# Moved operands and weights at fixed distances modulo 256 bytes: two kinds of slots in a one-core decoder step

## The chip, the cores and the metric

The kernel runs on one core of a Trainium2 chip. The metric is the device time of one execution in microseconds (us); lower is better. Times come from the runs and from one execution that the hardware profiler took.

## What is computed

One inference step of a one-layer decoder over 288 tokens: a prompt of 256 and 8 samples of 4 tokens. All is fp32. The reference, cut to the parts that matter here:

```python
mod = (silu(c) @ w_ada + b_ada)            # 6 vectors of 2048 for each of 9 groups
h = _rms(x, g_mix) * (1 + sc_m) + sh_m
proj = h @ w_in                            # 2048 -> 9216, split in seven
...                                        # short gated convolution; chunked spatial gating
merged = sigmoid(ga) * (ya @ w_pa) + sigmoid(gb) * (yb @ w_pb)
x = x + gt_m * (merged @ w_out)
h2 = _rms(x, g_ffn) * (1 + sc_f) + sh_f
gate, up = split(h2 @ w_ffn_in)            # 2048 -> 2 x 5632
x = x + gt_f * ((silu(gate) * up) @ w_ffn_out)
```

## The kernel before

Activations lie transposed: 128 features on the partitions, 288 tokens along the free axis. A matmul keeps a 128x128 piece of weights in the array and moves 128x288 of activations through it into one PSUM buffer (L229 to L234, in `triple`). For accuracy every fp32 operand is split in a high part (rounded to the format fp32r) and a low part (the rest), and a product is three matmuls: high weights with the high operand (L229), high weights with the low operand (L232), low weights with the high operand (L234). Each loads its weights anew.

The weights stream from HBM as blocks of up to 1 MB into seven `raw` buffers, on SP's queue in program order. For every four pieces, ScalarE (ACT) casts the high part into a `hi` tile (L453) and VectorE (DVE) subtracts for a `lo` tile (L459); there are four tiles of 2,048 bytes a partition of each (`SPB`). The moved operands are split likewise by `split` (L301, L303) and by `modulate` and `make_h1`, into tiles of the pool `slots`, named `s` in the profile.

The pool has 92 slots, all alike: they hold moved operands, but also evicted results, the partial sums of w_in (`part`) and small constants. A slot has room for `TU` = 298 columns, because the first stages move ten columns beside the tokens. The allocator rounds 1,192 bytes up to 1,216, so that slots begin at 32, 96, 160 or 224 modulo 256; the `hi` and `lo` tiles all begin at 224.

The order: conditioning vectors (`ada`, L393: fp32 matmuls spread over the stages), w_in in passes over parts of the depth (`wA`, `wB`, `wX`, `wS`, `wC`, `wE`, `wF`, `wD`), mixers, `pa`, `pb`, `wo`, then the FFN (`fk`, `fi`, and `f0` to `f3`). TensorE's order is written out by hand in the whole kernel. ACT, DVE and SP are recorded by hand in the first stages and are otherwise placed by the scheduling layer, which makes an instruction that writes a reused slot wait until its last reader is done.

In the first pass `sinkA` evicts each output tile from PSUM, for the first 48 (`ROOTLESS`) with the ten extra columns; `sinkC` and `rescale` read these columns later, once the root of the norm is known.

## Time and profile before

| | |
|---|---|
| median of 3 runs | 1624.26 us (1624.0 to 1624.49) |
| profiled execution | 1624.22 us, its span 1622.4 us |
| mean granted TensorE clock | 0.998 |
| TensorE busy | 1611.5 us, 12641 matmuls |
| DVE busy, ACT busy | 1017.0 us, 737.3 us |
| DMA | 357.88 MB, mean 221 GB/s |

The span runs from the first instruction to the last. A row of a group names source line, engine, operation and tiles (written <- read), then the shape and the count, busy time and the mean duration of one in ns. In a row of a window the columns are PE, PEld (weight loads), DVE, ACT and POOL busy in us with instruction counts, then the granted clock, the DMA share and GB/s; asked for one engine, it has that engine's column alone. Matmuls overlap: the next starts before the one ahead has drained, so the distance between starts (the pitch) is less than the duration of one.

### The profile page before, as it was taken

The numbers are of one execution on the slowest core, as the hardware profiler recorded it, in microseconds if no ns is written. First come the engines' busy times: TensorE is split into PE (matmuls) and PEld (weight loads), VectorE is DVE, ScalarE is ACT, GpSimd is POOL, SyncE is SP. The second block draws the span as 40 slices with busy tenths as digits, with TensorE's granted clock in tenths as the row PEclk, the third lists the DMA queues.
The fourth block names the chain that finished last, engine by engine and source line by source line (L and its number), as shares of the span: only waits on it lengthen the run. The fifth ranks groups of instructions, "written<-read, shape, count | busy, mean of one in ns | idle before, by whom it ended". The sixth has DMA issues, their size and how long they took to land.

```text
span 1622.4 us, 31579 instructions
## 1 busy us (share of the span) xinstructions
PE 1611.5 (99%) x12641; PEld 1547.6 (95%) x12641; DVE 1017.0 (63%) x2194; ACT 737.3 (45%) x1360; POOL 21.2 (1%) x65
## 2 busy tenths in 40 slices
PE   9999999999999999999999999999999999999997
PEld 8998999899999999999999999999999999999997
DVE  6676788877755667667744555555555555555565
ACT  5533344643444434456643444444444444444454
POOL 0000000000000000011000000000000000000000
PEclk9999999999999999999999999999999999999999
DMA  9887866777778676654576556443564534645341
GB/s 376 324 319 287 312 237 212 273 279 295 288 281 337 260 271 227 236 176 157 193 304 251 217 177 208 159 172 110 169 224 156 173 117 161 226 157 172 109 162 59
DMA packets 59476, 357.88 MB, mean 221 GB/s; under 512 B 6720, under 2 KB 10176, under 8 KB 28608
## 3 DMA queue, kind: packets, MB, share of 16 engines
q1 hardware_dynamic: 59040, 355.73, 59.8%
q8 instruction: 99, 1.62, 0.4%
q14 instruction: 49, 0.40, 0.1%
q10 hardware_dynamic: 288, 0.13, 0.0%
HBM read 352.74 MB, written 3.09 MB: 219 GB/s over the span
## 4 chain that ended last, share of the span: by engine, by line
PE 98%; DMA 1%; DVE 0%; ACT 0%; DVEq 0%; issue 0%; ACTq 0%
PE pm L229 31%; PE pm L234 30%; PE pm L232 30%; PE ada L393 5%; DMA raw<-in_wK 1%; DMA raw<-in_w 0%; DVE st L1048 0%; DMA ct<-in_c 0%; PE px L232 0%; PE px L229 0%; PE px L234 0%; PE px L880 0%; PE px L879 0%; PE px L826 0%; PE px L203 0%; ACT hi L453 0%
## 5 line engine op out<-in xcount | busy, mean ns | idle before, releaser
L229 PE MATMUL pm<-s,hi 128*128 128x288 f32 (+1 forms) x3750 | 1109.1, 296 | 0.0
L232 PE MATMUL pm<-s,hi 128*128 128x288 f32 (+1 forms) x3750 | 1103.8, 294 | 0.0
L234 PE MATMUL pm<-s,lo 128*128 128x288 f32 (+1 forms) x3738 | 1102.2, 295 | 0.0
L453 ACT CAST hi<-raw 128x512 fp32r<-128x512 f32 (+1 forms) x963 | 587.2, 612 | 803.3 <-PE pm L232 762.6
L459 DVE TENSOR_TENSOR lo<-raw,hi 128x512 fp32r<-128x512 f32 (+1 forms) x849 | 578.7, 683 | 437.9 <-ACT hi L453 425.3
L229 PEld LDWEIGHTS pm<-s,hi 128*128 128x128 f32 x3750 | 705.7, 188 | 15.2 <-issue 13.0
L232 PEld LDWEIGHTS pm<-s,hi 128*128 128x128 f32 x3750 | 704.7, 188 | 0.0
L234 PEld LDWEIGHTS pm<-s,lo 128*128 128x128 f32 x3738 | 702.9, 188 | 0.0
L248 DVE TENSOR_TENSOR lo<-raw,hi 128x512 fp32r<-128x512 f32 x111 | 74.6, 675 | 29.6 <-ACT hi L453 28.9
L393 PE MATMUL ada<-raw,cs 128*32 128x512 f32 (+2 forms) x1152 | 88.3, 452 | 0.2 <-DMA raw<-in_a 0.2
L393 PEld LDWEIGHTS ada<-raw,cs 128*32 128x32 f32 x1152 | 30.9, 110 | 45.0 <-issue 41.1
L771 DVE TENSOR_TENSOR s<-pm,s 128x288 f32<-128x288 f32 x72 | 32.8, 456 | 19.9 <-PE pm L234 19.7
L301 ACT CAST s<-t 128x288 fp32r<-128x288 f32 (+1 forms) x76 | 32.9, 433 | 18.8 <-DVE t L803 12.4
L303 DVE TENSOR_TENSOR s<-t,s 128x288 fp32r<-128x288 f32 (+1 forms) x76 | 34.9, 459 | 6.5 <-ACT s L301 6.4
L343 DVE SCALAR_TENSOR_TENSOR x<-pm,mod,x 128x256 f32<-128x256 f32 x79 | 37.6, 475 | 0.0
L969 DVE SCALAR_TENSOR_TENSOR t<-t,pm 128x288 f32<-128x288 f32 x42 | 19.1, 454 | 20.9 <-PE pm L234 20.9
L763 DVE TENSOR_TENSOR s<-pm,s 128x288 f32<-128x288 f32 x48 | 21.8, 454 | 10.4 <-PE pm L234 9.5
L342 DVE TENSOR_TENSOR t<-pm,mod 128x32 f32<-128x32 f32 x79 | 15.2, 192 | 18.3 <-PE pm L234 18.2
L748 DVE SCALAR_TENSOR_TENSOR s<-pm,s 128x256 f32<-128x256 f32 x48 | 23.1, 480 | 4.1 <-PE pm L234 4.1
L754 DVE TENSOR_TENSOR s<-s,rb 128x288 f32<-128x288 f32 x48 | 21.5, 448 | 0.0
L171 ACT ACTIVATE t<-x 128x288 f32<-128x288 f32 x29 | 12.9, 445 | 17.4 <-DVE x L346 17.4
L176 DVE TENSOR_TENSOR acc<-acc,t 128x288 f32<-128x288 f32 x33 | 15.0, 455 | 8.2 <-ACT t L171 8.2
(164 smaller groups left out, 470.9 us busy)
## 6 DMA issues: line engine op xcount, KB each, us to landing
raw<-in_fi SPq DMA_DIRECT2D x84, 1024.0 KB, 4.8
raw<-in_a SPq DMA_DIRECT2D x64, 1024.0 KB, 7.9
raw<-in_f SPq DMA_DIRECT2D x64, 704.0 KB, 4.0
raw<-in_wD SPq DMA_DIRECT2D x34, 1024.0 KB, 5.4
raw<-in_aE SPq DMA_DIRECT2D x16, 1024.0 KB, 9.6
raw<-in_wo SPq DMA_DIRECT2D x16, 1024.0 KB, 6.0
raw<-in_wC SPq DMA_DIRECT2D x19, 768.0 KB, 4.3
raw<-in_pa SPq DMA_DIRECT2D x8, 1024.0 KB, 5.9
```

The lines of the kernel that those rows point to most:

```text
L229: PE.matmul(out, wh, ah, start=first, stop=False)
L232: end_ = PE.matmul(out, wh, al, start=False, stop=turn and last)
L234: end_ = PE.matmul(out, wl, ah, start=False, stop=last)
L248: lows.pop(0)[1]()
L301: A.copy(hi, a)
L303: V.tensor_tensor(lo, a, hi.bitcast(F32), ALU.subtract)
L343: V.scalar_tensor_tensor(x[:, m, :TP], ps[:, :TP], mod[:, gt0 + m, 0:1], x[:, m, :TP], ALU.mult, ALU.add)
L393: PE.matmul(acc[32 * j : 32 * j + 32, :w], cs[:, kt, :], self.raw[:, o : o + w], start=kt == 0, stop=kt == 15, tile_position=(0, 32 * j), ...
L453: A.copy(hi, self.raw[:, s * 128 : e * 128])
L459: sub()
L748: V.scalar_tensor_tensor(t[:, :TP], ps[:, :TP], t[:, T : T + 1], t[:, :TP], ALU.add, ALU.add)
L771: V.tensor_tensor(a, ps[:, :T], a, ALU.add)
```

## The change

The pool of slots becomes two. 56 slots (`MAIN`) of `PITCH` = 320 columns, 1,280 bytes, hold the moved operands and what else is wide; 1,280 is five times 256, so all begin at the same place modulo 256. A moved operand (dtype fp32r) starts 7 columns, 28 bytes, into its slot (`LEADIN`). 36 slots of 288 columns (`KEPT`) hold the partial sums of 36 output tiles of w_in (`LONG`: 24 to 27 and 40 to 71), which live long. The twelve of these that have the ten extra columns put them into small tiles beside: `extra0`, `extra1` and `extra2`, 160 bytes a tile for four of them. `extra0` is allocated between the `hi` and the `lo` tiles and moves the `lo` tiles on by 160 bytes. By the layout of the built program every moved operand then lies 92 bytes from the high weights and 188 from the low ones, modulo 256; before it lay 0, 64, 128 or 192 bytes from both. `ct` and `ctt` move from constants of their own into the ring of temporaries.

```diff
-SLOTS = 92
+MAIN = 56
+KEPT = 36
+LEADIN = 7
+PITCH = 320
...
+LONG = tuple(range(24, 28)) + tuple(range(40, 72))
...
     def slot(dt=F32, shape=(P, T)):
-        return pslot.tile(list(shape), dt, tag="s", name=nm("s"), padded_shape=[P, TU])
+        o = LEADIN if dt == F32R else 0
+        t = pslot.tile([P, o + shape[1]], dt, tag="s", name=nm("s"), padded_shape=[P, PITCH])
+        return t[:, o:] if o else t
+
+    def kept():
+        return pkept.tile([P, T], F32, tag="k", name=nm("s"))
...
-    ct = const("ct", [P, 16, NC])
+    ct = tmp(16 * NC).rearrange("p (k n) -> p k n", n=NC)
...
+    extra, extra2 = [], const("extra2", [P, 4, TU - T])
+
+    def spare():
+        i = len(extra)
+        if i < 2:
+            extra.append(pw.tile([P, 4, TU - T], F32, tag=f"extra{i}", name=f"extra{i}", bufs=1))
...
                 hi = pw.tile([P, w], F32R, tag="hi", name=nm("hi"), bufs=SPB, padded_shape=[P, SEG * 128])
+                spare()
                 A.copy(hi, self.raw[:, s * 128 : e * 128])
                 lo = pw.tile([P, w], F32R, tag="lo", name=nm("lo"), bufs=SPB, padded_shape=[P, SEG * 128])
+                spare()
...
     def sinkA(m, ps):
-        t = slot(shape=(P, TU) if m < ROOTLESS else (P, T))
+        wide = m < ROOTLESS and m not in LONG
+        t = kept() if m in LONG else slot(shape=(P, TU) if wide else (P, T))
         part[m] = t[:, :T]
-        w = T
+        w = TU if wide else T
+        copy = A.copy if (m not in ON_VECTOR if m < ROOTLESS else m % 2 or m % 8 == 4) else V.tensor_copy
+        copy(t[:, :w], ps[:, :w])
         if m < ROOTLESS:
...
+            i = 0 if wide else LONG.index(m)
+            e = t[:, T:] if wide else (extra + [extra2])[i // 4][:, i % 4]
+            raws[m] = t, e
+            if not wide:
+                copy(e, ps[:, T:TU])
...
     def sinkC(m, ps):
...
-        V.scalar_tensor_tensor(t[:, :TP], ps[:, :TP], t[:, T : T + 1], t[:, :TP], ALU.add, ALU.add)
+        V.scalar_tensor_tensor(t[:, :TP], ps[:, :TP], e[:, :1], t[:, :TP], ALU.add, ALU.add)
```

The instructions of TensorE, POOL and SP keep their order and number. ACT and DVE have six more each. On ACT, in the first pass over w_in, this stands before the change; a number in a name counts the allocations of the build.

```order
L453 CAST hi_584<-raw_129 128x512
L740 COPY s_600<-pm_592 128x298
L453 CAST hi_609<-raw_129 128x512
L453 CAST hi_612<-raw_134 128x512
L740 COPY s_615<-pm_602 128x298
L589 ACTIVATE q_123<-x 128x1152
```

And after it:

```order
L471 CAST hi_590<-raw_133 128x512
L758 COPY s_606<-pm_598 128x288
L764 COPY extra_250<-pm_598 128x10
L471 CAST hi_616<-raw_133 128x512
L471 CAST hi_619<-raw_138 128x512
L758 COPY s_622<-pm_609 128x288
L764 COPY extra_250<-pm_609 128x10
L608 ACTIVATE q_127<-x 128x1152
```

Two evictions of output tiles (24 and 25) have become two copies each; all else keeps its place.

The second place is on ACT near the end of the product with w_out (`wo`), where pairs 13 and 14 of the 16 pairs of operands (`xg`) for the first blocks of the FFN are made; here the rows name in brackets what each waits for. Before:

```order
L935 ACTIVATE t_9513<-x,gm_90 128x256
L935 ACTIVATE t_9522<-x,gm_90 128x256 [waits Activation_49]
L301 CAST s_9518<-t_9513 128x298 [waits Activation_49,Pool_49]
L453 CAST hi_9533<-raw_8979 128x512 [waits DMAHW5_49,PE_49]
L301 CAST s_9527<-t_9522 128x298 [waits Activation_49,Pool_49]
L453 CAST hi_9537<-raw_8979 128x512 [waits PE_49]
```

And after:

```order
L957 ACTIVATE t_9531<-x,gm_93 128x256
L957 ACTIVATE t_9540<-x,gm_93 128x256 [waits Activation_49]
L311 CAST s_9536<-t_9531 128x298 [waits PE_49,Activation_49,Pool_49]
L471 CAST hi_9551<-raw_8997 128x512 [waits DMAHW5_49,PE_49]
L311 CAST s_9545<-t_9540 128x298 [waits Activation_49,Pool_49]
L471 CAST hi_9555<-raw_8997 128x512 [waits PE_49]
```

Nothing has moved, but the first cast into a slot now waits for TensorE too.

## The prediction

> **What bounds the kernel now.** I read the page first: its engine table, its slices and the chain that ended last.

> ```profile
> span 1622.4 us, 31579 instructions
> PE 1611.5 (99%) x12641; PEld 1547.6 (95%) x12641; DVE 1017.0 (63%) x2194; ACT 737.3 (45%) x1360; POOL 21.2 (1%) x65
> ...
> PE  9999999999999999999999999999999999999997
> ...
> PEclk9999999999999999999999999999999999999999
> ...
> PE 98%; DMA 1%; DVE 0%; ACT 0%; DVEq 0%; issue 0%; ACTq 0%
> ```

> TensorE is busy in every slice, at the full granted clock, and 98% of the chain lies on it. The waits view asks whether that busy row hides waiting:

> ```profile
> PE pm L576 <- POOL wb L570: 1.1, 1, 1.1
> PE px L203 <- DVE t L185: 0.6, 1, 0.6
> PE px L232 <- DVE s L692: 0.3, 1, 0.3
> ```

> It does not: the three longest waits for another engine come to 2.0 us. So the time is the number of matmuls times the distance from one start to the next. Three groups of the page hold nearly all of them, one for each product of a triple (L229: high weights by high operand, L232: high by low, L234: low by high). Below them is the windows view for a stretch of the FFN that holds only such matmuls.

> ```profile
> L229 PE MATMUL pm<-s,hi 128*128 128x288 f32 (+1 forms) x3750 | 1109.1, 296 | 0.0
> L232 PE MATMUL pm<-s,hi 128*128 128x288 f32 (+1 forms) x3750 | 1103.8, 294 | 0.0
> L234 PE MATMUL pm<-s,lo 128*128 128x288 f32 (+1 forms) x3738 | 1102.2, 295 | 0.0
> ```
> ```profile
> 1160.00:1340.00 180.00, 180.00 (x1363) 1.00 0.48 165
> ```

> 180.00 us over 1363 matmuls is a pitch of 132.1 ns. The groups hold 3750 + 3750 + 3738 = 11,238 matmuls, so 1 ns of pitch is worth 11.2 us. The "mean ns" of a row is longer than the pitch because matmuls are pipelined, but the two move together.

> What would the pitch be if nothing held a matmul up? The kernel contains the answer: the warm-up matmuls of L576 move 288 columns too, in bf16, from one unchanging operand. [...]

> ```profile
> L576 PE MATMUL pm<-wb x10: 286/286/287, 4.4 to 5.5; 128*128 128x288 bf16 x10
> L576 PEld LDWEIGHTS <-wb x8: 97/98/98, 4.6 to 5.4; 128*128 128x128 bf16 x8
> ```
> ```profile
> 4.43 1.14 PE L576 MATMUL pm<-wb 128*128 128x288 bf16 x8
> ```

> Eight matmuls in 1.14 us, the last of them 0.286 long: (1.14 - 0.286) / 7 = 122.0 ns of pitch at a duration of 286. The triples have 132.1 at a mean of (296 + 294 + 295) / 3 = 295. So about 10 ns of each, 113 us in all, is delay that 288 columns do not need by themselves. The line views of 800 to 1600 us show how it varies:

> ```profile
> L229 PE MATMUL pm<-s,hi x1980: 288/294/403, 800.0 to 1599.9; 128*128 128x288 f32 x198
> L232 PE MATMUL pm<-s,hi x1979: 288/295/303, 800.1 to 1599.7; 128*128 128x288 f32 x198
> L234 PE MATMUL pm<-s,lo x1980: 288/295/300, 799.8 to 1599.8; 128*128 128x288 f32 x198
> L229 PEld LDWEIGHTS pm<-s,hi x1980: 186/188/193, 799.8 to 1599.8; 128*128 128x128 f32 x198
> ```

> Each product has cases of 288, nearly free, and cases of 300 and more. Is that chance? A block of the FFN's first half goes through the same 16 pairs of operands in the same order, so I looked at the same two matmuls of a block (the low operand's product of the 14th pair, the first product of the 16th) in blocks 647 us apart, through the groups of a window 1 ns wide: first the one at 874.09 us, then the one at 874.74.

> ```profile
> L232 PE MATMUL pm<-s,hi 128*128 128x288 f32 x1 | 0.3, 288 | 0.0
> ```
> ```profile
> L229 PE MATMUL pm<-s,hi 128*128 128x288 f32 x1 | 0.3, 302 | 0.0
> ```

> The windows at 1520.75 and 1521.39 us give these two rows again, digit for digit. Shape, clock and work around are alike; what stays with the place in the block is where the operands lie. While a matmul reads its moved operand, the next weights are loaded (188 ns of record beside a pitch of 132), so two streams read SBUF at once, and the delay depends on where they stand to each other.

> **The change part by part.** By the layout of the two built programs, before: slots of 1,216 bytes, moved operands at 0, 64, 128 or 192 bytes modulo 256 from the weights, each about a quarter of the time. After: 92 from the high weights, 188 from the low ones, always.

> *The pitch.* No row shows a distance of 92 or 188, so the price is bounded by the rows above. I map durations to pitch linearly: 286 is 122.0, 295 is 132.1, 1.12 ns for each. Best end: no delay, 10.1 ns saved in 11,238 matmuls, -113 us. The best place of every product, 288, is 124.2 ns: 7.9 x 11,238 = -89 us. Worst end: 302 everywhere is 139.9 ns: +88 us. The mean of before is zero. I take 290, 126.5 ns: 5.6 x 11,238 = **-63 us**. Why nearer to the best row: on the grid of 64 bytes the delay changes from matmul to matmul and each starts in the state that the last one left; with one relation a triple repeats itself, and a delay that comes from the streams meeting is then either met three times in each triple or kept out. Two distances that fit the two kinds of weights separately leave no product on a place of its own. This is a judgement between bounds, not a measured price.

> *Twelve tiles lose their ten extra columns to a separate copy* (output tiles 24 to 27 and 40 to 47): 12 more evictions, of 128x10, six on ACT and six on DVE. The nearest rows:

> ```profile
> L974 ACT COPY w<-pm 128x9 f32<-128x9 f32 x3 | 0.4, 160 | 0.0
> L740 ACT COPY s<-pm 128x288 f32<-128x288 f32 x15 | 5.9, 394 | 0.0
> L740 ACT COPY s<-pm 128x298 f32<-128x298 f32 x25 | 10.1, 413 | 5.4 <-PE pm L234 4.3 <-PE pm L514 1.1
> ```
> ```profile
> L789 DVE COPY zout<-t 128x2 f32<-128x2 f32 x8 | 1.3, 165 | 0.0
> ```

> 160 - (413 - 394) = 0.14 us more on ACT for each and about 0.16 on DVE: 0.9 and 1.0 us. The cover is idle time there and four PSUM buffers:

> ```profile
> 60.00:100.00 40.00, 18.47 (x39) 1.00 0.79 304
> ```

> That is ACT alone, 18.47 of 40 us busy. On the path: 0, bounds 0 and 2 us.

> *Fewer common slots, 56 instead of 92.* Near the end of the product with w_out a cast of ACT gets a wait for TensorE: a slot is free only when an operand of the last block is done. Behind it on ACT stand the casts of the next weights, and DVE and TensorE wait for those. A block there is 48 matmuls, 6.3 us, and four weight buffers hold 16 triples, again 6.3 us.

> ```profile
> 745.00:765.00 20.00, 20.00 (x152) 20.00 (x152) 13.93 (x30) 12.64 (x28) 3.28 (x13) 1.00 0.47 159
> ```

> ACT is 12.64 us of 20 busy (fourth engine column). I take 0, bounds 0 and 2 us. If that cover were gone, the casts of the xg operands would be late next.

> *c and its tanh in the temporary ring, constants moved:* no instruction more; the rows of TensorE, POOL and SP keep their order, DMAs included. 0.

> *A faster TensorE asks more of its feeders.* DVE is fullest here:

> ```profile
> 200.00:400.00 200.00, 199.41 (x1532) 185.73 (x1531) 160.74 (x422) 93.64 (x175) 0.85 (x1) 1.00 0.69 259
> 20.00:60.00 40.00, 39.66 (x342) 37.77 (x342) 31.42 (x66) 28.08 (x60) 1.23 (x1) 1.00 0.93 363
> ```

> 80% becomes 84% with 4% more speed; still covered. From 20 to 60 us the DMA engines are at 0.93: those 342 matmuls may gain nothing, 342 x 5.6 ns = 1.9 us, given back.

> Sum: the profiled execution took 1624.22 us (span 1622.4 and 1.8 around it; median of the runs 1624.26). 1624.2 - 63 + 2 = **1563 us**.

> **The rivals.**

> *The one relation is a bad one (slower).* Same mechanism, other sign: the constant place costs more than the mixture. It decides at a mean duration of 295. At 297 the pitch is 134.3: 2.2 x 11,238 = +25 us, 1649; at worst 302, 1712. For it: rows of 300 and more exist for each product, and no row excludes 92 or 188. Against it: the medians lie at 294 and 295, so half of the sampled places are better than the mean already. 0.09.

> [...] 0.03. [...]

> *The place does not matter (no change).* If reading weights and moved operands don't touch each other, the 10 ns belong to the data type, and relations change nothing: 1624, plus or minus 3. Against it: 288 and 302 at fixed places of a block, with the same type. For it: the floor that I use is a bf16 row, with weights loaded in 98 ns, not 188. 0.07. [...]

> **How the numbers follow.** The forecast with whatever part of the gain: 0.81; the rivals 0.09, 0.03 and 0.07. The predicted time is the forecast's, 1563. The range starts at 1520, just above the bound without any delay (1624 - 113 = 1511), and ends at 1619, a pitch of 131.6; it leaves out the rivals (0.19) and little else. A measurement of this kernel tells 0.2% (3 us) from no change: faster 0.81, same 0.07, slower 0.12.

> **What would show it.** Right: the three product groups near 290 instead of 295, nearly the same in every block, with minimum and median of a line a few ns apart; 1420 or so matmuls instead of 1363 in 180 us of the FFN; waits of TensorE still some 2 us. Wrong: medians at 295 (place without effect), or one narrow value above it (a bad place); TensorE waiting for ACT around 755 us (slots) or for DVE before 400 us (feeders).

## The result and the profile after

The changed kernel takes 1596.22 us (median of 4 runs, 1596.16 to 1596.45) against 1624.26: 28 us less, a ratio of 0.9828 with a 95% interval of 0.9811 to 0.9845. The forecast of 1563 had the sign and the place right, and more than twice the gain (61 us). The profiled execution has a span of 1594.5 us. Its page first: the span, the busy time of each engine, TensorE and its clock in 40 slices, and the chain that ended last.

```profile
span 1594.5 us, 31602 instructions
...
PE 1583.4 (99%) x12641; PEld 1518.7 (95%) x12641; DVE 1015.9 (64%) x2200; ACT 735.7 (46%) x1366; POOL 20.9 (1%) x65
...
PE   9999999999999999999999999999999999999997
...
PEclk9999999999999999999999999999999999999999
...
PE 97%; DVE 2%; issue 0%; ACT 0%; DVEq 0%; POOL 0%; ACTq 0%; POOLq 0%
```

The picture is that of before: the same 12,641 matmuls, a mean granted clock of 0.998, 97% of the chain on TensorE. TensorE is busy 28.1 us less (1611.5 to 1583.4), which is the whole gain. The waits of TensorE for other engines are as small as before, 2.2 us in the three longest; a wait of 0.3 us for DVE now stands at another place:

```profile
PE pm L595 <- POOL wb L589: 1.1, 1, 1.1
PE px L213 <- DVE t L195: 0.8, 1, 0.8
PE pm L239 <- DVE s L998: 0.3, 1, 0.3
```

So the matmuls themselves come closer together. The three product groups of the page (the mean duration in ns stands behind the comma), and the line views from 800 us on (minimum/median/maximum):

```profile
L239 PE MATMUL pm<-s,hi 128*128 128x288 f32 (+1 forms) x3750 | 1095.4, 292 | 0.3 <-DVE s L998 0.3
L242 PE MATMUL pm<-s,hi 128*128 128x288 f32 (+1 forms) x3750 | 1090.6, 291 | 0.1
L244 PE MATMUL pm<-s,lo 128*128 128x288 f32 (+1 forms) x3738 | 1088.1, 291 | 0.0
```
```profile
L239 PE MATMUL pm<-s,hi x1987: 290/291/394, 799.9 to 1582.4; 128*128 128x288 f32 x199
L242 PE MATMUL pm<-s,hi x1987: 290/291/291, 800.1 to 1582.5; 128*128 128x288 f32 x199
L244 PE MATMUL pm<-s,lo x1988: 290/291/292, 799.8 to 1582.6; 128*128 128x288 f32 x199
L239 PEld LDWEIGHTS pm<-s,hi x1986: 186/187/188, 800.2 to 1582.2; 128*128 128x128 f32 x199
```

Before, a product had durations from 288 to 303; now the medians are 291, and two of the products stay within 2 ns over some 2,000 matmuls each. The windows view of 1000 to 1560 us, which holds only matmuls of triples in both kernels (start, length, TensorE's busy time with its count, clock, DMA share, GB/s), first of before, then of after:

```profile
1000.00:1560.00 560.00, 560.00 (x4235) 1.00 0.47 162
```
```profile
1000.00:1560.00 560.00, 560.00 (x4322) 1.00 0.48 164
```

560 us over 4235 is a pitch of 132.2 ns, over 4322 it is 129.6. Over 11,238 matmuls this difference of 2.66 ns would be 29.9 us; 28.0 were measured, so the stages outside this stretch gained a little less.

### The profile page after: what moved, and what is told of

It is laid out like the page before. It is cut to its first block, busy times and chain, and to the rows that moved or that the text cites. A ratio compares the mean times of both kernels' runs of the same rounds, so it can differ in the third digit from the quotient of the medians.

```text
span 1594.5 us, 31602 instructions
## 1 busy us (share of the span) xinstructions
PE 1583.4 (99%) x12641; PEld 1518.7 (95%) x12641; DVE 1015.9 (64%) x2200; ACT 735.7 (46%) x1366; POOL 20.9 (1%) x65
## 2 busy tenths in 40 slices
PE   9999999999999999999999999999999999999997
## 4 chain that ended last, share of the span: by engine, by line
PE 97%; DVE 2%; issue 0%; ACT 0%; DVEq 0%; POOL 0%; ACTq 0%; POOLq 0%
PE pm L239 30%; PE pm L244 30%; PE pm L242 30%; PE ada L403 5%; DVE lo L478 1%; PE pm L595 1%; DVE s L337 0%; DVE st L1070 0%; DVE s L318 0%; DVE t L331 0%; PE px L902 0%; ACT hi L471 0%; PE px L901 0%; PE px L213 0%; PE px L848 0%
## 5 line engine op out<-in xcount | busy, mean ns | idle before, releaser
L239 PE MATMUL pm<-s,hi 128*128 128x288 f32 (+1 forms) x3750 | 1095.4, 292 | 0.3 <-DVE s L998 0.3
L242 PE MATMUL pm<-s,hi 128*128 128x288 f32 (+1 forms) x3750 | 1090.6, 291 | 0.1
L244 PE MATMUL pm<-s,lo 128*128 128x288 f32 (+1 forms) x3738 | 1088.1, 291 | 0.0
L770 DVE SCALAR_TENSOR_TENSOR s<-pm,s 128x256 f32<-128x256 f32 x36 | 17.3, 481 | 2.7 <-PE pm L244 2.7
```

Source lines behind the costliest of these rows:

```text
L239: PE.matmul(out, wh, ah, start=first, stop=False)
L242: end_ = PE.matmul(out, wh, al, start=False, stop=turn and last)
L244: end_ = PE.matmul(out, wl, ah, start=False, stop=last)
```

## The experiments

Pitches below are worked out in this way: for a whole kernel from its count in 1000 to 1560 us, for a group of the benches from the start of one group to the start of the next, over its matmuls. Where many groups are compared (counts, means, extremes), the first eleven matmuls of each are left out, and the rest is called its steady part. Runs of the kernel before beside these experiments had medians of 1624.43 and 1624.3 us. bench, grid and forms ran once each.

**The price of each distance, measured by itself (bench).** After the last store of the changed kernel stand 9,216 matmuls that read lying data and whose products are used nowhere; its total time is not compared with anything.

```python
def group(name, pairs, n):
    out = pps.tile([P, 512], F32, tag="main", name=name, bufs=4)
    for i in range(n):
        w, o = pairs[i % len(pairs)]
        PE.matmul(out[:, :T], w, b[:, o : o + T], start=True, stop=True)

for i, c in enumerate(names):                    # 64 distances, 4 bytes apart
    group("one" + c, [(hi, i)], 48)              # always the same weights
for i, c in enumerate(names):
    group("tri" + c, [(hi, i), (hi, i), (lo, i)], 48)   # the operand 96 bytes further from lo than from hi
...                                              # and an 8 x 8 grid of both distances
```

> The changed kernel with 9,216 matmuls more after its last store, of the same shape and type, on a tile that is only read. 64 groups of 48 matmuls with one and the same weights, the moved operand 0, 4, 8 ... 252 bytes from them; 64 groups of triples with the step between high and low weights as in the kernel (d from the high, d + 96 from the low); 64 groups of triples on a coarse grid of both. Place theory (the distance sets the pitch): the groups differ by 5 ns and more, each steady in itself, and the triples with d = 92 show the kernel's 129.6 ns; a best distance lies near 124 to 126. Uniformity theory (any one relation that never changes gives the same): all groups within 1 ns of 129.6. Floor theory (129.6 is what a matmul of this type needs at best): no group below 129.

The timeline of TensorE (start, length, line, tile) around the triples at 84/180 (`triav`), 88/184 (`triaw`), 92/188 (`triax`) and 96/192 bytes (`triay`):

```profile
2134.02 6.76 PE L1046 MATMUL triav<-bench 128*128 128x288 f32 x48
2140.62 6.57 PE L1046 MATMUL triaw<-bench 128*128 128x288 f32 x48
2147.02 6.38 PE L1046 MATMUL triax<-bench 128*128 128x288 f32 x48
2153.24 6.54 PE L1046 MATMUL triay<-bench 128*128 128x288 f32 x48
2159.62 0.57 PE L1046 MATMUL triaz<-bench 128*128 128x288 f32 x3
```

Between starts lie 6.60, 6.40, 6.22 and 6.38 us for 48 matmuls: 137.5, 133.3, 129.6 and 132.9 ns. The third is the kernel's pitch, on data that nobody writes, where the program has nothing for DVE and ACT and the DMA share is 0.00 (1594 to 2000 us of this run), so the relation alone gives it. By the steady parts this is the lowest of the 64 distances of the triples and 84/180 with 137.9 the highest; their mean is 133.3, above the 132.2 of the mixture before, and only 18 of the 64 lie below it. So one relation everywhere is no gain in itself. It is a matter of which one. The place theory was right that the groups differ, and wrong in its best of 124 to 126: no group lies below 129, as the floor theory had it.

The distance modulo 16 orders them in part (means over 16 distances each, steady parts): 131.5 ns at 12, 132.6 at 0, 133.9 at 8, 135.2 at 4. No distance of the class of 4 lies below 132.2.

**The whole kernel with other lead-ins (lead0, lead8, lead5).** One number is changed. All moved operands still share one relation.

```diff
-LEADIN = 7
+LEADIN = 0        # lead0: 64 from the high weights, 160 from the low ones
+LEADIN = 8        # lead8: 96 and 192
+LEADIN = 5        # lead5: 84 and 180
```

> The changed kernel with moved operands at the start of their slots: 64 bytes from the high weights and 160 from the low ones, again one relation for all. Place theory: another steady pitch than 129.6, between 126 and 136 (1555 to 1668 us), and durations with less than 2 ns between minimum and median. Uniformity theory: 1596 us, within 3.

> The changed kernel with moved operands 32 bytes into their slots: 96 from the high weights and 192 from the low ones, 4 bytes further than the change. [...] If the place counts smoothly: within 0.5 ns of 129.6, 1591 to 1602 us. Uniformity theory: 1596 us.

lead0 took 1626.06 us (8 runs, 1624.39 to 1626.83; ratio to before 1.001, 0.9999 to 1.0022), lead8 1631.38 us (4 runs; 1.0044, 1.0024 to 1.0064). Four bytes further than the change, and 35 us are lost. The same window as above, lead0 and then lead8:

```profile
1000.00:1560.00 560.00, 560.00 (x4226) 1.00 0.48 162
```
```profile
1000.00:1560.00 560.00, 560.00 (x4216) 1.00 0.48 162
```

These are 132.5 and 132.8 ns. One relation for all does not by itself give 129.6 ns, so the uniformity theory falls with both runs. The bench's price holds for lead8 (132.9), and the 3 ns between 92/188 and 96/192 are not what a smooth dependence on the place would give.

For lead0 it holds only in parts: the bench had 131.1 for 64/160, and had the kernel held it throughout, lead0 would have gained 12 us. The kernel has two steady pitches at this one relation. Here is lead0 from 670 to 750 and from 1000 to 1080 us, which hold triples alone, then the third product in each of these windows, then the group of the bench at 64/160:

```profile
670.00:750.00 80.00, 80.00 (x612) 1.00 0.49 167
1000.00:1080.00 80.00, 80.00 (x605) 1.00 0.48 162
```
```profile
L244 PE MATMUL pm<-s,lo x204: 289/289/289, 670.1 to 749.9; 128*128 128x288 f32 x102
L244 PE MATMUL pm<-s,lo x202: 295/295/296, 999.8 to 1079.7; 128*128 128x288 f32 x101
```
```profile
L1046 PE MATMUL triaq<-bench x48: 289/292/298, 2102.1 to 2108.3; 128*128 128x288 f32 x48
```

From first to last start the pitch is 131.1 ns in the first window, the bench's, and 132.6 in the second. In the first the durations 296, 293 and 289 come again in every triple, as in the bench; in the second the pattern repeats itself after nine matmuls only. From 800 us on, lead0 stays in the second. The place theory foresaw a steady pitch, but one alone, and durations within 2 ns; they run from 291 to 298 in the second window. So this one relation has two steady pitches, and the bench showed one of them, 131.1; what decides between the two, the runs don't show. The line views of lead8 correct a reading of the prediction:

```profile
L239 PE MATMUL pm<-s,hi x1945: 293/296/402, 799.9 to 1589.7; 128*128 128x288 f32 x195
L242 PE MATMUL pm<-s,hi x1945: 289/295/298, 800.1 to 1589.8; 128*128 128x288 f32 x195
L244 PE MATMUL pm<-s,lo x1946: 293/294/303, 799.8 to 1590.0; 128*128 128x288 f32 x195
```

Here every triple has the same places, and durations still run from 289 to 303, at a pitch of 132.8. So a single short duration is not the mark of a good place, nor a single long one that of a bad place: they are steps in a pattern that, in the trace of lead8, repeats itself after fifteen matmuls, and only the mean step of the whole pattern is a price.

The bad end of the bench was then put into the kernel:

> After with a lead-in of 20 bytes in place of 28: moved operands 84 bytes from the high weights and 180 from the low ones, in every triple. Nothing else differs. Theory (a relation that repeats itself in every triple has its own steady price, and the price of the bench holds in the kernel): 84/180 had 137.9 ns in the bench, 8.3 above 129.6, so 1596.2 + 8.3 x 11,238 = 1689 us, some 65 us slower than before, every product line near 299. Rival A (the bench, which reads data that lie still, overstates bad places; 64/160 had 131.1 there and 132.3 in the kernel, nearer to the mean of all): 133 to 134, 1634 to 1645 us. [...]

lead5 took 1684.09 us (2 runs, 1684.0 and 1684.18; ratio 1.0368, 1.0337 to 1.0398): 60 us slower than before and 88 slower than the change, by 8 bytes. Its window and its three product groups:

```profile
1000.00:1560.00 560.00, 560.00 (x4066) 1.00 0.48 163
```
```profile
L239 PE MATMUL pm<-s,hi 128*128 128x288 f32 (+1 forms) x3750 | 1135.4, 303 | 0.0
L242 PE MATMUL pm<-s,hi 128*128 128x288 f32 (+1 forms) x3750 | 1135.0, 303 | 0.0
L244 PE MATMUL pm<-s,lo 128*128 128x288 f32 (+1 forms) x3738 | 1124.9, 301 | 0.0
```

560 / 4066 is 137.7 ns, 8.16 above the change, and 8.16 x 11,238 = 92 us against 88 measured. The theory's 1689 came within 5 us; rival A, with 1634 to 1645, fell.

**The pools and copies without the relation (mixed).** Slots of 304 columns, 1,216 bytes as before the change, which is no multiple of 256. The moved operands mix their places again, at multiples of 32; two pools, small tiles and the twelve divided evictions stay.

```diff
-LEADIN = 7
-PITCH = 320
+LEADIN = 0
+PITCH = 304
```

> The changed kernel with slots of 1,216 bytes again and no lead-in: moved operands at all multiples of 32 bytes from the weights, changing from matmul to matmul; the two pools, the twelve split evictions and the moved constants stay. Place and uniformity theory: the gain is gone, 1624 us within 6, pitch 132, durations from 288 to 302. If pools and copies made the gain: 1596 us.

It took 1625.43 us (8 runs, 1625.07 to 1626.2; ratio 1.0006, 0.9995 to 1.0017).

```profile
1000.00:1560.00 560.00, 560.00 (x4238) 1.00 0.48 163
```

That is 132.1 ns. The gain is gone entirely, so it belongs to the relation; pools, copies and slot counts together come to 1 us here, with an interval that includes zero and ends below 3.

**Is there a better relation? (grid).** The bench again, with 16 distances from the high weights (12, 28, ... 252) by 16 from the low ones, in triples:

```python
for i in range(16):
    for j in range(16):
        o, dl = 3 + 4 * i, 3 + 4 * j             # in units of 4 bytes
        a = 1152 + (o - dl) % 64
        lo, m = b[:, a : a + 128], b[:, o : o + T]
        group(..., [(hi, m), (hi, m), (lo, m)], 36)
```

> The changed kernel with 9,216 matmuls more after its last store: 256 groups of 12 triples, distances from the high and from the low weights set apart, each one of 12, 28, 44 ... 252 bytes (the residue modulo 16 that was best in the first sweep). Floor theory in its weak form (no steady relation of this kernel's operands goes below 129.6): no group below 129, and 92 with 188 among the best few. If the floor is lower and the change just missed it: some groups at 126 to 128, worth 18 to 40 us in the kernel. If only the distance of one of the two counts: rows or columns of the grid alike.

By the steady parts none of the 256 is below 129.5 ns. The best are 188/44 and 188/140 at 129.54; 92/188 has 129.62, which is 1 us of kernel time and no more than 2 ns over the 24 steps that are read. Seven lie below 129.9, the mean is 131.4. With the operand 92 bytes from the high weights, the low weights alone, by their distance, take the pitch from 129.6 (188) to 133.3 (76): the operand's own place does not set it alone. With the 64 distances of the first bench there is no sign of a place at which the 4-byte operands come down to the 122.0 ns of the bf16 row.

**The second distance alone (both92).** Both small tiles go behind the low weights, which then lie 92 bytes from the moved operands too.

```diff
                 hi = pw.tile([P, w], F32R, tag="hi", ...)
-                spare()
                 A.copy(hi, self.raw[:, s * 128 : e * 128])
                 lo = pw.tile([P, w], F32R, tag="lo", ...)
                 spare()
+                spare()
```

> After with both small tiles extra0 and extra1 allocated behind the low weights, so that these lie where the high ones lie modulo 256: moved operands 92 bytes from both. Theory (floor: 129.5 is as low as any place goes, and a place that is good by itself needs no second distance of its own): the bench had 130.0 for 92/92, so 1596.2 + 0.4 x 11,238 = 1600 us. Rival (the prediction's reason: the distance of 188 from the low weights carries a part of the gain of its own, at least a third of 28 us): 1605 us or more.

It took 1600.77 us (2 runs, 1600.42 and 1601.11; ratio to before 0.9855, 0.9826 to 0.9883).

```profile
1000.00:1560.00 560.00, 560.00 (x4309) 1.00 0.49 164
```

560 / 4309 is 130.0 ns, the price of 92/92 in the grid. A second distance for the low weights is worth 4.5 of the 28 us; the other 23.5 come with 92 bytes from both.

**What the rest depends on (forms).** Groups of 48 with one thing changed at a time: the moved width, the columns of the weights, how far off the operand lies (+0 to +1024 bytes), which of the two weights is at a bad distance, and bf16 at 32 distances.

```python
group(f"wide{..}", [(hi, b[:, 23 : 23 + n])], width=n)            # 92 bytes; "bad": 100 bytes
group(f"cols{..}", [(b[:, 1024 : 1024 + n], b[:, o : o + T])])    # n = 128, 96, 64, 32
group("ownaa", [(w1, at_100), (w2, at_92)])   # w1 8 bytes behind w2: own distance 92, to the next weights 100 or 84
group("half" + c, [(c16[:, 2048:2176], c16[:, 8 * i + 6 : 8 * i + 6 + T])])   # bf16, 12 modulo 16 ("four": 4)
```

> The changed kernel with groups of 48 matmuls after its last store, at 92 bytes (130.0 ns in the sweep) and at 100 (136.7). (1) Moved width 160 to 512 columns: if every moved column waits, the excess over the clock grows in proportion to the width; if only the columns beside the weight load do, it is the same 7 and 14 ns at all widths. (2) Weights of 128, 96, 64 and 32 columns: if the load causes the excess, it shrinks with the columns, from 7 to about 2 ns at 92 and from 14 to 3 at 100; if not, it stays. (3) The moved operand 0, 256 ... 1024 bytes further: the same pitch within 1 ns if only the distance modulo 256 counts. (4) Two weights in turn, 92 from their own moved operands and 100 or 84 from those beside whose reading they are loaded, and the other way round: 136 and 130 ns if the load beside counts, 130 and 136 if a matmul's own weights do. (5) bf16 at 32 distances: 122.0 to 123 ns at all if the type has no excess; 125 and more at some if two reads meet there too.

The timeline at the width of 288 with 92 bytes and with 100; with 92 bytes and 32 columns of weights; and bf16 at 92. The row below each is the start of the next group.

```profile
1618.08 6.40 PE L1045 MATMUL wideaj<-bench 128*128 128x288 f32 x48
1624.32 0.45 PE L1045 MATMUL wideak<-bench 128*128 128x320 f32 x2
...
1689.86 6.72 PE L1045 MATMUL badaj<-bench 128*128 128x288 f32 x48
1696.42 0.76 PE L1045 MATMUL badak<-bench 128*128 128x320 f32 x4
...
1759.92 6.40 PE L1045 MATMUL colsaxab<-bench 128*32 128x288 f32 x48
1766.16 0.56 PE L1045 MATMUL colsazae<-bench 128*128 128x288 f32 x3
...
1898.39 6.06 PE L1045 MATMUL halfaf<-benchb 128*128 128x288 bf16 x48
1904.29 0.41 PE L1045 MATMUL halfag<-benchb 128*128 128x288 bf16 x2
```

- 6.24 / 48 = 130.0 ns at 92 and 6.56 / 48 = 136.7 at 100, 6.7 more.
- With weights of 32 columns, whose load is recorded with 107 ns and not 187, it is 130.0 as well. So the 130.0 does not hang on the recorded length of the weight load. At 100 bytes the short load saves 3.3 of the 6.7 ns, but not in the order of its length: 96 columns have 133.3 as well, 64 have 135.0.
- bf16: 5.90 / 48 = 122.9, and 122.5 to 122.9 at all 32 distances (12 and 4 modulo 16, the best and the worst class above). For bf16 these places have no price beyond 0.4 ns. At every place sampled the triples of 4-byte operands take some 7 ns more than that, 129.5 and up.
- The difference between 100 and 92 bytes does not grow with the width: 2.1 ns at 256 columns, 6.7 at 288, 2.6 at 320, 6.7 at 448, 3.9 at 512. A price for every moved column would grow; this one goes up and down. At 224 columns both have 111.7, and 160 and 192 at 100 bytes have no less.
- 256 to 1,024 bytes further, nothing changes (130.0 at 92 and 136.7 at 100 each time): at these two distances only the place modulo 256 counts.
- A good distance to a matmul's own weights and a bad one to the next gives 133.3, the other way round 135.9; the expectation had 136 and 130 one way or the other. Neither distance decides alone.

## Why the prediction was half right

- **What bounds the kernel, and the mechanism:** right. No wait (2.2 us in the three longest), no clock (0.998 granted before and after), no feeder; the place of the operands modulo 256 moves the pitch, from 129.6 ns (92/188) to 137.7 (84/180, lead5). mixed takes the relation away and the gain with it; lead5 turns it into a loss. That 92/188 of all distances came out lowest of the 64 in the bench is luck: nothing in the prediction singled it out.
- **The duration of 290:** nearly right. The groups came out at 292, 291 and 291, narrow as described. In the 180 us of the FFN there were 1391 matmuls, not some 1420.
- **The step that failed is the line from duration to pitch,** "286 is 122.0, 295 is 132.1, 1.12 ns for each", and with it the term of -63 us, 5.6 ns of pitch, which measured 2.66 ns and 28 us. Its lower end is a bf16 row, and forms shows none of this delay for bf16 (122.5 to 122.9 ns at 32 distances). Between kernels of 4-byte operands the line is flatter: lead5 has 137.7 at a mean of 302.3, after 129.6 at 291.3, so 8.16 / 11.0 = 0.74 ns for each. By that, 290 would have been 128.6 and the gain 3.6 x 11,238 = 40 us instead of 63; the 1.3 ns by which the durations missed 290 take 11 of these away, which leaves 29; 28 were measured. The "10 ns of delay that 288 columns do not need" were 2.7 that a place can save and some 7 that no place sampled saves.
- **The best end, "the best place of every product, 288":** a misreading. lead8 shows 289 in a relation that is slower than the mixture, and the change, with no duration below 290 from 800 us on, is faster. A single matmul's duration is no price; only the pitch of a repeated pattern is.
- **The reason for going nearer to the best row,** that one relation keeps the delay out or meets it three times: not borne out. The one relation of lead0 came out at 132.5, no better than the mixture of before, and 46 of the 64 triples in the bench lie above the mixture. Nor does one relation make every triple repeat the last: lead0's second pattern takes three triples, lead8's five.
- **"Two distances that fit the two kinds of weights separately":** worth 4.5 us (both92).
- **Copies, slots, feeders:** 0 was right (mixed, 1 us). The twelve small copies took 1.1 us on ACT and 0.9 on DVE, close to the 0.9 and 1.0 priced:

```profile
L764 ACT COPY extra<-pm x6: 168/174/187, 31.6 to 52.9; 128x10 f32<-128x10 f32 x6
L764 DVE COPY extra<-pm x6: 157/158/160, 34.8 to 53.9; 128x10 f32<-128x10 f32 x6
```

  No wait of TensorE for ACT is longer than 0.2 us, so the one feared around 755 us did not come. The stretch from 20 to 60 us, from which nothing was expected, gained its 2% as well: 349 matmuls instead of 342.

```profile
20.00:60.00 40.00, 39.73 (x349) 37.79 (x348) 32.02 (x75) 28.43 (x65) 1.23 (x1) 1.00 0.93 367
```

- **The rivals.** A bad relation did not come, but it was likelier than 0.09 for a relation that one knows nothing of: by the bench nearly three in four are worse than the mixture. The bound given for it, 1712, holds lead5's 1684. "The place does not matter" is refuted for the 4-byte operands (129.6 to 137.9 ns in the triples of the bench) and agrees with the bf16 rows (122.5 to 122.9 ns at 32 distances). No run shows a cost behind the 0.03 that is part of the 0.12 for slower; measured, the distances of 12 modulo 16, to which 92 belongs, are the best class and better than the multiples of 16 (131.5 against 132.6 ns).

What stays open: what the 7 ns are that 4-byte operands take above bf16 at every place sampled (129.5 against 122.9), since no matmul of this type was run without its weight load; why, of the distances of one class modulo 16, some are 130 and some 133; and what sets lead0 on one or the other of its two pitches. That the weight load and the reading of the moved operand get into each other's way is argued from the dependence on their distance (129.6 ns at 92/188, 137.5 at 84/180); no run takes one of the two away.

## What to carry to other kernels

Where matmuls of 4-byte operands stand back to back and each loads its weights, lay the moved operands and the weights out on a pitch that is a multiple of 256 bytes (in forms, 256 to 1,024 bytes more left 130.0 and 136.7 ns as they were), and choose their distance by a bench of some dozens of matmuls for each place: the places sampled here spread over 6% of the pitch (129.5 to 137.9 ns), on both sides of the mixture. Then measure the choice in the kernel: of the five relations tried in both, four kept the bench's price, and lead0 kept it in parts only. Before you price such a change, take the floor from rows of the same data type (129.5 ns here, against 122.0 in the bf16 row), and the price from the pitch of a repeated pattern, never from the shortest single duration (lead8 has 289 at a pitch of 132.8). Padding that makes all places alike without choosing which may well lose (lead8 7 us, lead5 60).
